# Third phase of a hybrid encoder trunk: order of one load, engine of one copy, place of two projections

## The chip, the cores and the metric

The kernel runs on one core of one Trainium2 chip. The metric is the device time of one execution in microseconds (us), the median of the runs shown. A core has five engines that each work through their own list of instructions: TensorE (PE in the profile, matmuls and transposes into PSUM; its weight loads are listed as PEld), VectorE (DVE), ScalarE (ACT), GpSimd (POOL) and SyncE (SP, which here issues most of the transfers). They wait for one another by semaphores.

## The reference

Two independent sequences of 1024 tokens with 1024 channels go through one layer with the same weights. The layer normalises its input, projects it to four branches (a gated linear recurrence, chunked gated linear attention "GLA", chunked gated DeltaNet, and a diagonal complex state-space model "S5"), mixes the four results with sigmoid gates and projects them back. The part that matters here is GLA and S5. GLA, cut to its core, for each of four heads and both directions:

```python
b = jnp.cumsum(log_a, axis=2)                      # log_a from a rank-16 projection of the input
q_dec, k_inv = q * jnp.exp(b), k * jnp.exp(-b)
scores = jnp.where(causal, q_dec @ k_inv.T, 0.0)   # inside a chunk
o_intra = scores @ v
S = de * S + k_end.T @ v                           # state carried from chunk to chunk
o = o_intra + q_dec @ S
o = rms_norm(o, norm_g) * silu(gate)
```

q, k, v and the gate are column blocks of one projection of the normalised input. S5 runs a complex linear scan over the sequence for 32 groups of channels; the kernel does it in real arithmetic after turning each state by a precomputed rotation.

## The kernel before, in words

The sequences are handled one after the other (`s` = 0, 1), each in four phases. A phase opens PSUM banks and buffers of its own and weaves several Python generators together. The weave (`weave`) gives every generator a position between 0 and 1; it always advances the one that lies furthest back, and a generator moves on by the number it yields, divided by its declared total. So a generator that yields less reaches its later parts earlier among the others.

The order that this writes is not yet the order on the engines. The framework takes the written order as a priority, runs a planning model of the engines over it, and fixes each engine's list for good: at each step the earliest written instruction that the plan holds to be ready. On the chip an engine keeps to its list, and stands still when the instruction in front is not ready, whatever lies behind it. Buffers are handed out in the same pass; a new user of a buffer waits for the last reader of the old one.

Every projection is done in float32 precision by three passes: a weight block is loaded (`raw`, two buffers), ScalarE rounds it (`hi`), GpSimd subtracts (`lo`), and TensorE adds up hi*hi, lo*hi and hi*lo products. `hi` and `lo` have four buffers each; one projection of 128 columns uses two, `values` (256 columns) all four. Results go to three PSUM banks called `pj`.

The third phase weaves three things: `gla` (declared total 18), `s5_core` (total 8, one unit for each of eight groups of four) and blocks of merge-gate projections for later ("gate blocks", `early`), six (first sequence) or seven (second) from position 0.3 on and seven from 0.85 on, each of 16 steps with three matmuls.

`gla` treats two pairs of heads (`pr` = 0, 1). Before the loop it projects q and k of the first pair (`qk(0)`) and starts the decays of the first direction. For each pair it then scales q and k of both directions by their decays (`scaled`), projects v (`values`: eight blocks of 128 tokens, each evacuated from its `pj` bank into the tile `vt`), builds the states for each direction (`states`: transposes of the scaled keys into a `gl` bank, a ScalarE copy to `kT`, the products of `kT` and `vt`, and VectorE's chain over the chunks into `Sm`), and forms the outputs (`outputs`: scores, mask, products, ScalarE copies). `ends` normalises the pair's outputs; for the first pair this is finished after the second pair's decays have begun. Its gate is loaded into a buffer with the tag `vt`, of which there is one, so the second pair's `vt` can be written only after the last read of that gate, the second `Sm<-gl,gla_ng,vt`. Between `states` and `outputs` of the first pair stand q and k of the second (`yield from qk(1)`), and the decays that follow.

q and k have one buffer each. `s5_core` loads, for each group of four, `uT` (the input, two buffers), `tin` (input weights, one buffer) and `E` (rotation and decay, two buffers), multiplies on TensorE into two `s5` banks (`head`), turns and scans on VectorE with products on GpSimd (`scan`), and multiplies back one group later (`tail`, a bank that ScalarE empties with a gelu into `zt`).

Nearly all instructions stand under line L54 in the profile, that of the helper that passes a call on, so they are told apart by tile names. Transfers have lines of their own: L1265 `uT`, L1266 `tin`, L1267 `E`, L202 weights.

Of the kernel before, what the change touches and what calls it, by code (L numbers as in the profile page):

```python
# [33 lines left out]
def tile_hybrid_trunk(ctx: ExitStack, tc: tile.TileContext, A):  # L34
# [28 lines left out]
    V, S, G, PE = Line(nc.vector, False), Line(nc.scalar, False), Line(nc.gpsimd, False), Line(nc.tensor)  # L63
    dma = nc.sync.dma_start
# [12 lines left out]
    def bank(tag):  # L77
        return ps["pool"].tile([128, 512], F32, tag=tag, bufs=ps["nb"][tag], name=nm(tag))
# [17 lines left out]
    def mm(*a, **kw):  # L96
        PE.matmul(*a, **kw)

    def transpose(*a):
        PE.transpose(*a)  # L100
# [4 lines left out]
    def tt(eng, out, a, b, op):  # L105
        eng.tensor_tensor(out, a, b, op)
# [7 lines left out]
    def stt(out, a, s, b, o1, o2):  # L114
        V.scalar_tensor_tensor(out, a, s, b, o1, o2)

    def bc(ap, n):
        return ap.unsqueeze(ap.ndim).to_broadcast(list(ap.shape) + [n])
# [4 lines left out]
    def nm(p):  # L123
        cnt[0] += 1
        return f"{p}{cnt[0]}"
# [103 lines left out]
    def run(gen):  # L229
        for _ in gen:  # L230
            pass
# [69 lines left out]
    def proj_cm(*a):  # L301
        run(proj_steps(*a))

    def proj_tok(xn, wp, src, c0, toks, evac):

        ws = wcols(wp, src, 0, 8, c0, 256)
        for i, tsl in enumerate(toks):
            p = bank("pj")
            n = 0
            for k in range(8):  # L310
                wh, wl = ws[k]
                xh, xl = xn[k][:, 0, tsl], xn[k][:, 1, tsl]
                for a, b in ((xh, wh), (xh, wl), (xl, wh)):
                    mm(p[:, :256], a, b, start=(n == 0), stop=(n == 23))
                    n += 1
            with soon():
                evac(i, p[:, :256])
# [554 lines left out]
    def gla(s, xn, ms, wp, pl):  # L872

        wt = lambda shape, tag, dt=F32: pl.tile(shape, dt, tag=tag, name=nm(tag))

        def qk(pr):
            q, k = wt([128, T], "q"), wt([128, T], "k")
            for t_, c0 in ((q, GLA_Q), (k, GLA_K)):
                def ev(hf, sl, p, t_=t_):
                    S.copy(t_[:, sl], p)  # L880
                proj_cm(xn, wp, w_in, c0 + pr * 128, 128, ev)
                yield
            return q, k

        def values(pr):
            vt = wt([128, 8, 256], "vt")

            def evv(i, p):
                V.tensor_copy(vt[:, i], p)
            proj_tok(xn, wp, w_in, GLA_V + pr * 256,  # L890
                     [slice(c * 128, (c + 1) * 128) for c in range(NT)], evv)
            return vt
# [34 lines left out]
            stt(q_, q, 0.125, Ab, ALU.mult, ALU.mult)  # L927
            return q_, k_, sm

        def states(d, k_, vt, sm):  # L930

            kT = wt([128, 8, 128], "kT")
            for g4 in range(2):
                p = bank("gl")
                for c in range(4):
                    cc = g4 * 4 + c
                    transpose(p[:, c * 128:(c + 1) * 128], k_[:, cc * 128:(cc + 1) * 128], ident)
                S.copy(kT[:, g4 * 4:g4 * 4 + 4], p.rearrange("p (c n) -> p c n", c=4))
            yield 0.4

            Smd = wt([128, 8, 128], f"Sm{d}")
            own = (slice(0, 4), slice(4, 7)) if d == 0 else (slice(4, 8), slice(1, 4))
            for cg in own:
                p = bank("gl")
                for c in range(cg.start, cg.stop):
                    for h in range(2):
                        o = (c - cg.start) * 128
                        mm(p[h * 64:(h + 1) * 64, o:o + 128], kT[:, c, h * 64:(h + 1) * 64],
                                  vt[:, c, h * 128:(h + 1) * 128], start=True, stop=True)
                n = cg.stop - cg.start  # L950
                sh = 1 if d == 0 else -1
                tt(V, Smd[:, cg.start + sh:cg.stop + sh], p[:, 0:n * 128].rearrange("p (c n) -> p c n", c=n),
                   bc(sm[:, 2, cg], 128), ALU.mult)
            for i in range(1, NT - 1):
                c = i if d == 0 else 7 - i
                cn = c + 1 if d == 0 else c - 1
                stt(Smd[:, cn], Smd[:, c], sm[:, 1, c:c + 1], Smd[:, cn], ALU.mult, ALU.add)
            use_c = slice(1, 8) if d == 0 else slice(0, 7)
            tt(V, Smd[:, use_c], Smd[:, use_c], bc(sm[:, 0, use_c], 128), ALU.mult)
            yield 0.4  # L960
            return Smd
# [44 lines left out]
            return [norm_out(pl, "gl", [ot[h]], gla_ng, sg[:, h], (s, 1, pr * 2 + h), wt([128, T], f"Sm{h}"),  # L1006
                             ot[h].rearrange("p c n -> p (c n)")) for h in range(2)]

        q, k = yield from qk(0)
        last = None  # L1010
        ab = decay(0, 0)
        yield 0.3
        for pr in range(2):
            one = scaled(0, q, k, *ab)
            ab = decay(1, pr)
            yield 0.3
            if last:
                for e in last:
                    run(e)
                yield 0.3  # L1020
            two = scaled(1, q, k, *ab)
            vt = values(pr)
            yield 2
            Sm = []
            for d, x in enumerate((one, two)):
                Sm.append((yield from states(d, x[1], vt, x[2])))
            if pr == 0:
                q, k = yield from qk(1)
                ab = decay(0, 1)
                yield 0.3  # L1030
            ot = yield from outputs((one[0], two[0]), (one[1], two[1]), Sm, vt)
            last = ends(pr, ot)
            for e in last:
                next(e)
            yield 0.3
# [8 lines left out]
    rot_d = dr.tile([NQ, 128, 3, 4, 128], F32, name="rot_d")  # L1044
# [16 lines left out]
    def s5_rot(rot, pl):  # L1061

        for qd in range(NQ):
            gs = slice(qd * 4, qd * 4 + 4)
            eng = V if qd % 2 == 0 else G
            E = pl.tile([128, 3, 4, 128], F32, tag="E", name=nm("E"))
            V.memset(E[:, 0, :, 0:1], 1.0)
            V.memset(E[:, 1, :, 0:1], 0.0)
            V.tensor_copy(E[:, 0:2, :, 1], rot[:, 0:3:2, 0, gs])
            for lv in range(1, 7):  # L1070
                m = 1 << lv
                both = [128, 2, 4, m]
                e, f = E[:, 0:2, :, 0:m], E[:, 0:2, :, m:2 * m]
                y = E[:, 2].rearrange("p a n -> p (a n)")[:, 0:8 * m].rearrange("p (r a n) -> p r a n", r=2, a=4)
                tt(eng, f, e, bc(rot[:, 0, lv, gs].unsqueeze(1).to_broadcast([128, 2, 4]), m), ALU.mult)
# [181 lines left out]
    def s5_core(s, xn, wp, pl):  # L1257
# [3 lines left out]
        def load(qd):  # L1261
            uT = wt([128, 4, 128], "uT", 2)
            tin = wt([128, 4, 2, 128], "tin")
            E = wt([128, 3, 4, 128], "E", 2)
            dma(uT, u_d[s, qd // 2, qd % 2 * 4:qd % 2 * 4 + 4].rearrange("g x c -> x g c"))  # L1265
            dma(tin, tin_d[qd])  # L1266
            dma(E, rot_d[qd])  # L1267
            return tin, uT, E

        def head(qd, tin, uT, E):  # L1270
# [308 lines left out]
    for s in range(nseq):  # L1579
        if s:  # L1580
            xn = last_part(s - 1, mg, me)
        with ExitStack() as br:
            fp = pool(f"fg{s}", 1, stack=br)
            bp = pool(f"bp{s}", 1, stack=br)
            with ExitStack() as st:
# [75 lines left out]
                pr = {}  # L1661
# [87 lines left out]
```

## Time and profile before

| what | value |
|---|---|
| median of 3 runs | 3104.76 us (3102.79 to 3108.0) |
| the profiled execution | 3103.76 us, its span 3101.5 us |
| mean granted TensorE clock | 0.966 of full speed |
| PE busy | 2875.3 us, 93% of the span |
| DVE busy | 1877.1 us, 61% |
| ACT busy | 1286.2 us, 41% |
| POOL busy | 1043.0 us, 34% |

[...] In a timeline, the bracket behind a row is the time that the engine stood idle before it, and what ended the wait. A name such as `vt<-pj` is the tile written and the tile read. The third phase's GLA lies at about 670 to 1010 us in the first sequence and 2145 to 2530 us in the second.

### The profile page before, as it was taken

Reading aid. Unit: us, or ns where it says so; the run is one execution under the profiler, and the core shown is the slowest. Engines: PE = TensorE matmul, PEld = TensorE weight load, DVE = VectorE, ACT = ScalarE, POOL = GpSimd, SP = SyncE. Lnnn points to the kernel's source line nnn. Section 1 sums busy time; section 2 is a strip of 40 time slices with the busy share of each in tenths; the row PEclk is TensorE's granted clock in tenths of the full one; section 3 lists DMA queues with packets and bytes.
Section 4 is the critical chain, followed back from the end, with each engine's and each line's share of the span. In section 5 each row is a group of like instructions: output and inputs, shape, how many; then the busy total and the mean of one; then the engine's idle time right before and its main releaser. Section 6 shows DMA issues by size and latency. Waiting matters only on the chain. (4 is left out here: it accounts for less than half of the span.)

```text
span 3101.5 us, 42101 instructions
## 1 busy us (share of the span) xinstructions
PE 2875.3 (93%) x15386; PEld 2373.6 (77%) x15386; DVE 1877.1 (61%) x3569; ACT 1286.2 (41%) x1969; POOL 1043.0 (34%) x796
## 2 busy tenths in 40 slices
PE   6999979898989999999999998989897999999998
PEld 5787767677778787878778876767776887788877
DVE  7576887738662464665654467773867245566545
ACT  5644546534432432332444465553443233333223
POOL 2343565434332231121443333343433212211123
PEclk9999989999999999999999998999998999999999
DMA  5344535353332754553553342524333263565343
GB/s 111 102 153 142 153 104 182 92 162 121 121 112 74 214 162 157 176 194 124 182 160 109 102 137 73 165 80 160 117 120 104 74 192 104 183 216 192 105 156 124
DMA packets 449391, 427.37 MB, mean 138 GB/s; under 512 B 126848, under 2 KB 340384, under 8 KB 449184
## 3 DMA queue, kind: packets, MB, share of 16 engines
q1 hardware_dynamic: 403200, 374.07, 39.2%
q10 hardware_dynamic: 45984, 50.61, 4.7%
q8 instruction: 121, 1.98, 0.3%
q14 instruction: 86, 0.70, 0.1%
HBM read 306.87 MB, written 117.70 MB: 137 GB/s over the span
## 5 line engine op out<-in xcount | busy, mean ns | idle before, releaser
L54 PE MATMUL pj<-xn,hi 128*128 128x512 f32 x4608 | 1471.2, 399 | 20.2 <-ACT y L54 5.7
L54 POOL TENSOR_TENSOR lo<-raw,hi 128x512 fp32r<-128x512 f32 x432 | 600.9, 1394 | 1451.8 <-ACT hi L54 1298.3
L54 PEld LDWEIGHTS pj<-xn,hi 128*128 128x128 f32 x4608 | 869.7, 191 | 206.1 <-ACT y L54 6.1
L54 PE MATMUL pj<-xn,lo 128*128 128x512 f32 x2304 | 912.5, 396 | 1.3 <-POOL lo L54 1.3
L54 ACT CAST hi<-raw 128x512 fp32r<-128x512 f32 x432 | 265.2, 618 | 650.8 <-PE pj L54 482.2
L54 PEld LDWEIGHTS pj<-xn,lo 128*128 128x128 f32 x2304 | 439.5, 191 | 99.5 <-issue 5.0
L54 ACT ACT_TABLE_LOAD x201 | 257.9, 1283 | 118.2 <-DVE Ab L54 54.6
L54 PE MATMUL pj<-yh,hi 128*128 128x512 f32 x576 | 239.8, 417 | 4.5 <-ACT yh L54 4.4
L54 PE MATMUL pj<-yl,hi 128*128 128x512 f32 x576 | 225.8, 393 | 1.0 <-DVE yl L54 1.0
L54 PE MATMUL pj<-yh,lo 128*128 128x512 f32 x576 | 226.0, 393 | 0.0
L54 DVE TENSOR_TENSOR_SCAN w<-E,v 64x512 f32<-64x512 f32 x64 | 97.9, 1529 | 85.2 <-PE s L54 84.3
L54 DVE TENSOR_TENSOR sg<-sg,pj 128x512 f32<-128x512 f32 x128 | 87.6, 684 | 93.4 <-PE pj L54 65.6
L54 PE MATMUL pj<-hi,mh 128*128 128x512 f32 x384 | 124.3, 400 | 6.7 <-ACT mh L54 4.1
L54 PEld LDWEIGHTS pj<-yh,hi 128*128 128x128 f32 x576 | 109.6, 190 | 23.9 <-ACT yh L54 5.2
L54 PEld LDWEIGHTS pj<-yh,lo 128*128 128x128 f32 x576 | 108.7, 189 | 23.8
L54 PEld LDWEIGHTS pj<-yl,hi 128*128 128x128 f32 x576 | 109.5, 190 | 19.9 <-DVE yl L54 2.6
L54 ACT ACTIVATE fg<-pj,bmg 128x512 f32<-128x512 f32 x112 | 76.3, 687 | 116.4 <-PE pj L54 104.2
L54 ACT ACTIVATE vn<-r,beta 128x128 f32<-128x128 f32 x128 | 40.7, 365 | 169.5 <-DVE vs L54 167.3
L54 POOL TENSOR_TENSOR dcv<-dcv,dsg 128x1024 f32<-128x1024 f32 x24 | 60.4, 2518 | 144.3 <-ACT dsg L54 103.5
L54 PE MATMUL pj<-hi,xn 128*128 128x256 f32 x512 | 97.9, 290 | 10.0 <-DVE vt L54 10.0
L54 DVE TENSOR_TENSOR yl<-yr,yh 128x512 fp32r<-128x512 f32 x80 | 59.9, 753 | 76.3 <-ACT yh L54 76.1
L54 DVE SCALAR_TENSOR_TENSOR dcv<-dup,dn_cw,dcv 128x1024 f32<-128x1024 f32 x72 | 96.0, 1333 | 5.5 <-ACT dcv L54 2.5
(373 smaller groups left out, 4469.1 us busy)
## 6 DMA issues: line engine op xcount, KB each, us to landing
raw<-in_w_in_dram SPq DMA_DIRECT2D x176, 256.0 KB, 2.9
sl<-rows_d SPq DMA_DIRECT2D x128, 256.0 KB, 6.5
raw<-in_w_merge_gate_dram SPq DMA_DIRECT2D x128, 256.0 KB, 2.9
gs_d<-fg ACTq DMA_DIRECT2D x112, 256.0 KB, 2.1
sg<-gs_d SPq DMA_DIRECT2D x112, 256.0 KB, 2.7
sl<-qkv_d SPq DMA_DIRECT2D x40, 512.0 KB, 5.5
raw<-in_w_branch_dram SPq DMA_DIRECT2D x64, 256.0 KB, 3.4
yr<-ysp SPq DMA_DIRECT2D x64, 256.0 KB, 3.1
```

The costliest lines, as they stand in the source:

```text
L54: i = f(*a, **kw)
```

## The change

Three edits in the third phase. `qk` puts its two tiles on a list instead of returning them, and for the first pair an iterator over `qk(1)` is handed to `states`, which advances it once for each direction, after the transposed keys have been copied out and before its own yield: q of the second pair is projected there in the first direction, k in the second. These steps yield nothing to the weave. The loop runs what is left of the iterator where `yield from qk(1)` stood; the sum of what `gla` yields falls from 19.1 to 17.1. `values` evacuates with a ScalarE copy instead of a VectorE copy. In `load`, E is requested first.

```diff
+        qks = []
+
         def qk(pr):
...
-            return q, k
+            qks.append((q, k))
...
             def evv(i, p):
-                V.tensor_copy(vt[:, i], p)
+                S.copy(vt[:, i], p)
...
-        def states(d, k_, vt, sm):
+        def states(d, k_, vt, sm, ahead):
...
                 S.copy(kT[:, g4 * 4:g4 * 4 + 4], p.rearrange("p (c n) -> p c n", c=4))
+            next(ahead, None)
             yield 0.4
...
-        q, k = yield from qk(0)
+        yield from qk(0)
+        q, k = qks[0]
...
+            ahead = qk(1) if pr == 0 else iter(())
             for d, x in enumerate((one, two)):
-                Sm.append((yield from states(d, x[1], vt, x[2])))
+                Sm.append((yield from states(d, x[1], vt, x[2], ahead)))
             if pr == 0:
-                q, k = yield from qk(1)
+                run(ahead)
+                q, k = qks[1]
                 ab = decay(0, 1)
                 yield 0.3
...
+            dma(E, rot_d[qd])
             dma(uT, u_d[s, qd // 2, qd % 2 * 4:qd % 2 * 4 + 4].rearrange("g x c -> x g c"))
             dma(tin, tin_d[qd])
-            dma(E, rot_d[qd])
```

## Rows read from the trace of the kernel before

**Rows 1.** The page's busy line: us, share of the span, instructions.

```profile
PE 2875.3 (93%) x15386; PEld 2373.6 (77%) x15386; DVE 1877.1 (61%) x3569; ACT 1286.2 (41%) x1969; POOL 1043.0 (34%) x796
```

**Rows 2.** Busy time by stretches of the third phase, with columns.

```profile
core 0: us, PE busy (x) PEld busy (x) DVE busy (x) ACT busy (x) POOL busy (x), PEclk, DMA share, GB/s
670.00:865.00 195.00, 184.91 (x1112) 156.39 (x1112) 131.62 (x218) 81.65 (x110) 74.14 (x45) 0.97 0.36 112
865.00:885.00 20.00, 10.62 (x55) 10.39 (x56) 19.67 (x30) 5.01 (x7) 7.75 (x4) 0.66 0.53 170
885.00:1057.00 172.00, 171.83 (x982) 144.00 (x981) 71.86 (x145) 47.62 (x71) 45.47 (x32) 1.00 0.40 127
2340.00:2375.00 35.00, 13.19 (x84) 12.61 (x85) 33.42 (x58) 6.48 (x8) 13.73 (x8) 0.72 0.42 140
```

**Rows 3.** PE's waits, whole span: total us, times, longest.

```profile
PE gl L54 <- ACT kT L54: 10.4, 2, 5.2
PE s L54 <- DVE t L54: 5.8, 2, 2.9
```

**Rows 4.** Timeline of PE, first sequence, first pair's states: start, us, what.

```profile
737.39 0.69 PE L54 MATMUL gl<-vt,kT 128*64 128x128 f32 x2 [5.21 <-ACT kT L54]
738.01 3.45 PE L54 MATMUL s<-uT,tin 128*128 128x128 f32 x16
753.70 0.49 PE L54 MATMUL s<-uT,tk 128*128 128x128 f32 x2 [2.91 <-DVE t L54]
```

**Rows 5.** Groups on PE from 727.7 to 737.3 us.

```profile
L54 PE MATMUL pj<-xn,hi 128*128 128x512 f32 x14 | 4.4, 396 | 0.0
L54 PE MATMUL pj<-xn,lo 128*128 128x512 f32 x6 | 2.3, 391 | 0.0
```

**Rows 6.** Timeline of ACT before that wait ends.

```profile
717.89 0.70 ACT L54 ACTIVATE Rl<-gl,gla_bn 128x512 f32<-128x512 f32 x1
...
736.26 0.60 ACT L54 ACTIVATE zt<-s 128x512 f32<-128x512 f32 x1
736.76 0.58 ACT L54 COPY kT<-gl 128x512 f32<-128x512 f32 x1
```

**Rows 7.** Stretches behind two of the waits, columns as in rows 2.

```profile
735.00:740.00 5.00, 2.61 (x11) 2.29 (x12) 4.96 (x4) 3.33 (x5) 3.80 (x2) 0.50 0.21 54
880.00:885.00 5.00, 4.41 (x23) 4.41 (x24) 4.76 (x14) 0.00 (x0) 0.00 (x0) 0.57 0.51 157
```

**Rows 8.** Timeline of DVE, then PE, first sequence, between the pairs.

```profile
874.66 1.41 DVE L54 SCALAR_TENSOR_TENSOR Sm<-gl,gla_ng,vt 128x512 f32<-128x512 f32 x2
875.99 2.02 DVE L54 TENSOR_TENSOR ki<-k,Rl 128x1024 f32<-128x1024 f32 x1
...
880.13 1.07 DVE L54 COPY vt<-pj 128x256 f32<-128x256 f32 x3
...
880.59 0.58 PE L54 MATMUL pj<-hi,xn 128*128 128x256 f32 x1 [5.45 <-DVE vt L54]
```

**Rows 9.** The same place in the second sequence, DVE, then PE.

```profile
2370.08 2.01 DVE L54 TENSOR_TENSOR ki<-k,Rl 128x1024 f32<-128x1024 f32 x1
2372.01 1.07 DVE L54 COPY vt<-pj 128x256 f32<-128x256 f32 x3
...
2358.18 0.76 PE L54 MATMUL s<-uT,tk 128*128 128x128 f32 x2 [15.02 <-issue]
```

**Rows 10.** The copies' forms: duration ns min/median/max, first and last start.

```profile
L54 DVE COPY vt<-pj x32: 390/417/425, 706.7 to 2388.7; 128x256 f32<-128x256 f32 x32
L54 ACT COPY qd<-gl x16: 349/373/374, 818.9 to 2510.6; 128x256 f32<-128x256 f32 x16
```

**Rows 11.** E's issues and time to landing, and the first product of the inputs.

```profile
L1267 SPq DMA_DIRECT2D E<-rot_d x16: 319/320/1114, 636.8 to 2352.0; - x16
DMA to landing us min/median/max: 3.5/4.3/10.4
L54 PE MATMUL s<-uT,tin x256: 270/275/582, 681.8 to 2367.2; 128*128 128x128 f32 x128
```

## The prediction
> **What bounds the kernel.** I read the page's busy line first, then PE's busy time and granted clock by stretches, then PE's waits, and last the timelines around the longest waits. TensorE is busy 93% of the span [rows 1], so the end moves only by what PE stands idle or runs at half clock. In the third phase the reader should see three kinds of stretch [rows 2]. From 670 to 865 us, pair 0 of the first sequence, PE has 184.91 of 195 us. At the border between the pairs it falls apart: 10.62 of 20 us at clock 0.66 in the first sequence, 13.19 of 35 us at 0.72 in the second, with DVE busy 19.67 and 33.42 us. After the border, from 885 to 1057 us, PE has 171.83 of 172 us, and there nothing can be gained. Two of PE's waits come once in each sequence with the same length [rows 3]: 10.4 us in two for `kT`, 5.8 us in two for the S5 scan. VectorE and ScalarE count only where PE waits for them.
>
> The order on each engine is fixed beforehand from the written order and planned times. So an edit has two effects: what a thing costs, and where the plan puts it. The second I can only bound.
>
> **v evacuated by ScalarE.** 32 copies leave VectorE at 0.417 us and come to ScalarE at 0.373 us, the price of a copy of the same shape out of PSUM [rows 10]: 13.3 us of VectorE, 11.9 us of ScalarE. ScalarE is busy 41% [rows 1], and a copy is hidden as long as a `pj` bank is free, so only places where PE waits count.
>
> First sequence, between the pairs [rows 8]: the last read of the old gate, which frees `vt`, ends at 874.66 + 1.41 = 876.07 us. The copies start at 880.13 us, behind two long VectorE instructions for the second direction, and PE goes on at 880.59 us after 5.45 us idle. ScalarE has finished its last `kT` copy by then and could copy at 876.07: 4.06 us saved. Second sequence [rows 9]: the buffer is free at about 2370.1 us, where `ki` starts, and the copies start at 2372.01 us: 1.9 us saved. Behind the first gap PE runs 4.41 busy us at clock 0.57 [rows 7], which loses about 0.43 x 4.41 = 1.9 us; with the gap cut to some 1.4 us I take half of that back, 1.0 us.
>
> Against it: in pair 0 the copies of late v blocks fall into ScalarE's chain for the second direction's decay, which runs without a gap from before 717.89 us [rows 6]. Two of them add 2 x 0.373 = 0.75 us, and VectorE loses one copy of 0.417 us from the same chain further down: +0.33 us, in each sequence +0.7 in all if PE feels it. What waits behind a v copy on ScalarE is the `kT` copy, the gelu and the roundings of weights. Sum: -4.1 - 1.9 - 1.0 + 0.7 = -6.3 us. If ScalarE turns out as late as VectorE was, it is +0.7; if the clock comes back wholly, -7.2.
>
> **q and k between transposed keys and products.** The work is the same, 2 x 48 matmuls in each sequence; it moves ahead of two waits. In pair 0 PE does the transposes, then 20 gate matmuls in the free time (14 + 6, some 4.6 us, 0.23 us each) [rows 5], then stands 5.21 us until `kT` [rows 4], which ScalarE copies at 736.76 us because `zt`, the gelu of S5's tail, goes at 736.26 us after the decays' exponentials [rows 6]. After it PE runs at clock 0.50 [rows 7]: the 16 input products at 738.01 take 3.45 us [rows 4], 1.5 to 1.9 us lost. One projection is 48 x 0.23 = 11 us, more than the 9.8 us (4.6 + 5.21) between the transposes and `kT`. If PE does all of q first, the gap and its clock go: 5.2 + 1.9 = 7.1 us per sequence, 14.2 us in all.
>
> What is late next: the input products of the next S5 group are written before the transposes, so they keep precedence over q. They need the bank that `zt` empties at 736.26 + 0.60 = 736.86 us. If the plan holds that bank to be free as early as now, PE reaches them after 20 matmuls as before and waits till 736.9: 0.5 us gained where 5.2 went. And the tail at 753.70 us waits 2.91 us for VectorE's scan [rows 4]; its end does not come earlier, so what PE gains before it is lost there, unless k, also 11 us, stands in front of it. From both sides the edit is worth 0 to -14.2 us for the `kT` gap, and at most -5.8 us more for the tails [rows 3]. The nearest rows are those of the same waits, and they show both releases (ScalarE at 736.86, VectorE at 753.7) untouched, so I take a value near the lower end: 2.5 us per sequence, -5.0 us.
>
> The q and k tiles have one buffer each; their new contents can be copied only after the second direction's scaling has read the old. That comes before the scan that the tail waits for, within q's 11 us, and two of the three banks hold both halves meanwhile: 0, at worst about one copy, 0.6 us as for `kT` [rows 6].
>
> **The fall of the yielded sum from 19.1 to 17.1.** All of `gla` after `qk(1)` comes 2/18 = 0.11 of the phase earlier against S5 and the gate blocks: about one S5 group and one gate block of 11 us move behind the border. Between the first outputs and the second values I count two gate blocks before and after, so the border has as much cover as it had. The second sequence's border stands 21.8 us idle (35 - 13.19) against 9.4 us (20 - 10.62) in the first [rows 2], 15.02 us of it before one S5 tail [rows 9]: it may fall to the first's pattern, -12.4 us, or not. I take 0, as nothing in the code decides it.
>
> **E first.** E lands 4.3 us after its issue (3.5 to 10.4) [rows 11]; ahead of `uT` and `tin` it can delay these by that much, but at the phase's start they are issued with E, near 636.8 us, and first used at 681.8 us [rows 11]. Later each of the three waits for its own buffer. No engine's wait ends with E's landing, so nothing is gained: 0, with up to 10 us of delay inside 40 us of cover.
>
> **Sum.** -6.3 - 5.0 = -11.3 us. The profiled execution took 3103.76 us, 2.26 us of it outside the span of 3101.5; it lies 1.0 us under the median. 3103.8 - 11.3 = 3092.5, on the median's scale 3093.5 us.
>
> **Rivals.**
>
> *The stall only moves (no change).* For it: PE's order follows planned times, and the releases that it waits for, `zt` and the scan, are not moved; v's gain at the border may be taken by the S5 scan that is now written ahead of the second direction's scaling. Against: the 4.06 us at the border is VectorE's queue and nothing else. 3104.8 - 2 = 3103 us.
>
> *The border closes too.* The second sequence's border falls to the first's pattern, -12.4, and q takes half of its upper end, -7.1, beside v's -6.3: 3104.8 - 25.8 = 3079 us. For it: both borders run the same code, and one is 12.4 us shorter. Against: VectorE is busy 33.42 of 35 us there and loses only copies of 0.417 us.
>
> *The cover is missing later (slower).* Pair 1 had a gate block written among its transposes and products; `gla` now passes there 0.11 earlier, so transposes and products of pair 1 stand without a block between them, as in pair 0 before. PE was without idle time there [rows 2]. If each sequence gets pair 0's `kT` gap with its clock there, 7.1 us, and the tail's 2.9 us [rows 4], that is +20.0, with v's -6.3 and q's 0: 3104.8 + 13.7 = 3118.5 us. It decides once the plan puts the products within less than 9.8 us of work behind the transposes. Against: seven gate blocks from 0.85 on are there to be drawn forward, and the decays of pair 1 are over by then, so ScalarE is freer. [...]
>
> **How the numbers follow.** A measurement here can tell about 0.2%, 6.2 us, from no change. Forecast (3086 to 3098) 0.40, border closes too 0.17, stall moves 0.26, slower 0.17. Faster by over 6.2 us: the first two, 0.57; within it 0.26; slower 0.17. The lower end takes in the upper bounds of the known waits, -7.2 - 14.2 - 12.4 = -33.8, rounded: 3072. The upper end goes half-way into the slower case, 3112, and leaves out about 0.15 in all. The likeliest case's own range is 3086 to 3098.
>
> **What would show it.** Right: no `vt<-pj` copy on VectorE, PE's wait for it at both borders under 2 us, and PE's `kT` waits gone in pair 0. If instead PE waits before `s<-uT,tin` or longer before the tail, the stall moved. Slower would show as new PE waits above 1 us after the border, where there were none. A wait of PE for `uT` that grows by some 4 us would make E's place matter. The forecast is wrong if PE's idle time in the third phase falls by less than 5 or more than 20 us, or if what it falls by comes back elsewhere.

## The result, and the profile after

The change made the kernel slower: 3121.72 us median (3117.36 to 3128.51, 4 runs) against 3106.38 us (3102.79 to 3108.57, 4 runs), a ratio of 1.0051 [1.0037, 1.0064], some 16 us. The forecast was 3093.5 us.

TensorE's busy line, against [rows 1], shows 20 us more busy time for the same 15386 matmuls, and VectorE not busier:

```profile
PE 2895.9 (93%) x15386; PEld 2389.1 (76%) x15386; DVE 1874.5 (60%) x3537; ACT 1290.6 (41%) x1997; POOL 1040.5 (33%) x796
```

The third phase of the profile after by stretches, columns as in [rows 2], PEclk being the granted TensorE clock as a share of full speed (this execution, the slowest of the four, is some 6 us late already when the phase begins):

```profile
670.00:860.00 190.00, 174.83 (x1022) 145.11 (x1021) 119.45 (x176) 78.61 (x112) 65.99 (x39) 0.96 0.33 104
860.00:900.00 40.00, 23.21 (x170) 22.60 (x169) 38.96 (x65) 10.01 (x15) 16.45 (x9) 0.79 0.43 138
900.00:1060.00 160.00, 160.00 (x882) 133.69 (x882) 59.26 (x102) 44.00 (x68) 44.10 (x32) 1.00 0.30 98
2340.00:2390.00 50.00, 31.87 (x221) 30.82 (x221) 46.24 (x80) 13.58 (x19) 17.33 (x9) 0.76 0.40 133
```

The reader is to see that most of the new idle time lies at the first sequence's border: TensorE has 23.21 of 40 us there at clock 0.79, while VectorE is busy 38.96. Behind the border PE has 160 of 160 us, as before. Idle time is only one side of the account: the 20 us of the busy line are the other, and most of the net loss lies there (the section on the second reading).

PE's waits after (total us, times, longest). The waits for `kT` [rows 3] are gone; the second row shown is the tail's, 12.7 us where it was 5.8:

```profile
PE s L54 <- issue: 17.9, 2, 13.0
...
PE s L54 <- DVE t L54: 12.7, 2, 6.4
...
PE gl L54 <- DVE qd L54: 9.9, 1, 9.9
...
PE s L54 <- ACT zt L54: 6.2, 2, 3.1
...
PE pj L54 <- ACT vt L54: 5.5, 2, 2.9
```

PE's timeline in the first sequence, only rows that follow a wait. The first three are pair 0 (for [rows 4]), the last three the border (for [rows 8]):

```profile
742.86 2.01 PE L54 MATMUL s<-uT,tin 128*128 128x128 f32 x8 [3.12 <-ACT zt L54]
...
759.60 0.77 PE L54 MATMUL s<-uT,tk 128*128 128x128 f32 x2 [6.37 <-DVE t L54]
...
815.29 1.19 PE L54 MATMUL gl<-Sm,qd 64*128 64x128 f32 x4 [4.41 <-DVE sc L54]
...
879.59 0.76 PE L54 MATMUL s<-uT,tk 128*128 128x128 f32 x2 [12.99 <-issue]
...
886.58 2.02 PE L54 MATMUL s<-uT,tin 128*128 128x128 f32 x16 [1.18 <-DMA uT<-u_d]
...
891.65 0.39 PE L54 MATMUL pj<-hi,xn 128*128 128x256 f32 x1 [2.62 <-ACT vt L54]
```

In pair 0, 5.21 + 2.91 us of waiting became 3.12 + 6.37, and the outputs wait 4.41 us for `sc`, where before has no wait of over 0.8 us. At the border 4.15 + 5.45 us became 12.99 + 1.18 + 2.62. The 4.15 us stand in this row of before:

```profile
868.93 2.82 PE L54 MATMUL gl<-ident,ki 128*128 128x128 f32 x12 [4.15 <-DVE ki L54]
```

"issue" names nothing, but VectorE's timeline does. This is VectorE at that border after the change:

```profile
854.25 1.21 DVE L54 TENSOR_TENSOR qd<-qd,rs 128x1024 f32<-128x1024 f32 x1
...
855.46 8.07 DVE L54 TENSOR_TENSOR_SCAN w<-E,v 64x512 f32<-64x512 f32 x4
863.56 1.09 DVE L54 TENSOR_SCALAR rs<-ssn 128x8 int32<-128x8 int32 x1
864.57 5.69 DVE L54 TENSOR_TENSOR_SCAN Ab<-ones,Rl 128x128 f32<-128x128 f32 x8
...
870.18 0.14 DVE L54 CAST rs<-rs 128x8 f32<-128x8 int32 x1
...
873.22 0.16 DVE L54 CAST rs<-rs 128x8 int32<-128x8 f32 x1
...
878.22 1.28 DVE L54 TENSOR_TENSOR t<-E,s 128x512 f32<-128x512 f32 x2
...
882.49 1.22 DVE L54 TENSOR_TENSOR ki<-ki,rs 128x1024 f32<-128x1024 f32 x1
883.90 5.85 DVE L54 TENSOR_TENSOR_SCAN w<-E,v 64x512 f32<-64x512 f32 x4 [0.19 <-PE s L54]
```

and before:

```profile
855.29 1.53 DVE L54 TENSOR_TENSOR qd<-qd,rs 128x1024 f32<-128x1024 f32 x1
856.75 0.16 DVE L54 TENSOR_SCALAR ssn<-ssn 128x8 f32<-128x8 f32 x1
...
867.65 1.22 DVE L54 TENSOR_TENSOR ki<-ki,rs 128x1024 f32<-128x1024 f32 x1
868.79 5.84 DVE L54 TENSOR_TENSOR_SCAN w<-E,v 64x512 f32<-64x512 f32 x4
```

The normalisation of the second head (`ends`) is a chain of some 15 steps (`ssn`, `rs`), all but one of 0.14 to 0.2 us, then `ki<-ki,rs`, whose transposes PE needs. Before, the chain ran first and S5's scan came behind it. After, the scan of an S5 group (8.07 us) and its products stand in the middle of the chain. From the start of `qd<-qd,rs` to the end of `ki<-ki,rs` it takes 883.71 - 854.25 = 29.5 us, before 868.87 - 855.29 = 13.6 us. Some of that is the scans themselves: the four of S5 took 8.07 us here and 5.84 us before, the eight of the decays (`Ab`) 5.69 us and 2.7 us; every long one of them (2.13 to 3.42 us for S5 where the others took 1.21 to 1.22, 1.41 to 1.42 us for the decays where the others took 0.39 to 0.42) began beside a GpSimd instruction (last section). PE's 12.99 us end 0.09 us after one of VectorE's reads of the S5 banks (878.22 + 1.28 = 879.50). S5 stands later against GLA than before: the fourth `zt` of the phase starts at 861.27 us, just ahead of the border, where before it started at 826.97 us and the fifth at 864.81 us.

The profile before has the same picture at the other border, and it was there to be read: the 15.02 us of [rows 9]. They end 0.09 us after such a read of VectorE too, and the chain takes 28.8 us there (2333.28 to 2362.09). The change brought the second sequence's border to the first, not the other way round. The second's own shrinks from 22.2 us of waits (1.50 + 15.02 + 1.11 + 4.54) to 17.8 (9.94 + 4.95 + 2.90). Over the two sequences idle time thus hardly changes: +9.1 and -7.6 us in the table below.

### The profile page after: what moved, and what is told of

Same layout as the page of the kernel before. It is cut to its first block, busy times and chain, and to the rows that moved or that the text cites. A ratio compares the mean times of both kernels' runs of the same rounds, so it can differ in the third digit from the quotient of the medians.

```text
span 3126.5 us, 42086 instructions
## 1 busy us (share of the span) xinstructions
PE 2895.9 (93%) x15386; PEld 2389.1 (76%) x15386; DVE 1874.5 (60%) x3537; ACT 1290.6 (41%) x1997; POOL 1040.5 (33%) x796
## 5 line engine op out<-in xcount | busy, mean ns | idle before, releaser
L54 PEld LDWEIGHTS pj<-yh,hi 128*128 128x128 f32 x576 | 108.7, 189 | 24.3 <-ACT yh L54 5.7
```

The costliest lines, as they stand in the source:

```text
L54: i = f(*a, **kw)
```

## Experiments

Each experiment was run in five rounds beside the kernel before on the same chip. To find where a profile gains or loses, I took the time between two of TensorE's matmuls of fixed number, counted by start: from the 3300th to the 5600th (third phase, first sequence) and from the 10850th to the 13000th (second), with PE's idle time in it in brackets. Every kernel runs the same 15386 matmuls, and their order is the same around those two ends.

| kernel | edit | ratio to before [95%] | first (idle), us | second (idle), us |
|---|---|---|---|---|
| before | | | 421.7 (23.8) | 410.3 (38.2) |
| after | all three | 1.0051 [1.0037, 1.0064] | 438.8 (32.9) | 411.1 (30.6) |
| e1_v | v on ScalarE alone | 0.9965 [0.9952, 0.9978] | 414.9 (18.1) | 407.8 (36.1) |
| e2_E | E first alone | 0.9996 [0.9985, 1.0007] | 422.1 (24.3) | 411.9 (39.0) |
| e3_qk | q, k moved, yields gone | 1.0070 [1.0054, 1.0087] | 440.7 (34.3) | 415.5 (35.6) |
| e4_shift | yields gone, nothing moved | 1.0060 [1.0046, 1.0074] | 437.6 (28.7) | 414.0 (33.0) |
| e5_all_keep | all three, yields kept | 1.0006 [0.9995, 1.0017] | 424.0 (23.0) | 408.0 (38.4) |
| e6_qk_keep | q, k moved, yields kept | 1.0030 [1.0018, 1.0041] | 431.6 (28.1) | 408.9 (36.9) |
| e16_q_only | only q moved, kept | 1.0026 [1.0016, 1.0036] | 425.2 (26.6) | 414.1 (41.2) |
| e17_q_second | q into the second place | 0.9998 [0.9990, 1.0007] | 421.2 (23.4) | 409.1 (35.9) |
| e7_s5rate | after, S5 faster throughout | 1.0064 [1.0049, 1.0079] | 439.6 (27.1) | 413.8 (31.1) |
| e14_s5_back | after, S5 set back | 1.0062 [1.0050, 1.0075] | 438.1 (31.9) | 420.0 (38.5) |
| e15_gates_back | after, gate blocks set back | 1.0106 [1.0088, 1.0123] | 441.1 (36.5) | 423.0 (47.8) |
| e18_both_back | after, both set back | 1.0041 [1.0028, 1.0054] | 437.5 (35.0) | 411.5 (37.8) |
| e8_v_joint | e1 with one norm chain | 0.9922 [0.9908, 0.9936] | 413.5 (17.7) | 396.0 (23.4) |
| e9_all_joint | after with one norm chain | 1.0026 [1.0013, 1.0039] | 431.1 (25.6) | 409.0 (30.6) |
| e19_keep_joint | e5 with one norm chain | 0.9959 [0.9945, 0.9973] | 426.1 (22.4) | 393.7 (21.2) |
| e11_all_pair | after, two heads tied | 1.0070 [1.0058, 1.0082] | 442.8 (42.7) | 412.9 (41.3) |
| e12_v_joint_pair | e8, two heads tied | 0.9958 [0.9946, 0.9970] | 418.8 (25.0) | 402.9 (29.5) |
| e13_all_joint_pair | e9, two heads tied | 1.0032 [1.0021, 1.0043] | 435.4 (34.0) | 406.7 (32.9) |

### The parts of the change, one at a time

v alone:

```diff
-                V.tensor_copy(vt[:, i], p)
+                S.copy(vt[:, i], p)
```

> Only the v copies on ScalarE; the order on TensorE is that of before. Theory A (the loss comes from gla reaching its later parts 2/18 earlier, which puts S5's scans into the border between the pairs): this edit is innocent and gives its own 4 to 6 us at the two borders, ratio 0.998. Theory B (the place of q and k itself loses): the same, 0.998. Theory C (v copies on ScalarE hold up what is queued behind them): slower by 5 us or more, 1.002 or above.

It gained 0.35%, more than the 0.2% expected. PE's waits for `vt` at the two borders fell from 5.45 to 1.11 and from 4.54 to 2.44 us:

```profile
880.37 0.39 PE L54 MATMUL pj<-hi,xn 128*128 128x256 f32 x1 [1.11 <-ACT vt L54]
...
2368.20 0.39 PE L54 MATMUL pj<-hi,xn 128*128 128x256 f32 x1 [2.44 <-ACT vt L54]
```

E alone, in `load`:

```diff
+            dma(E, rot_d[qd])
             dma(uT, ...)
             dma(tin, tin_d[qd])
-            dma(E, rot_d[qd])
```

> Of the change only the rotation's load first. TensorE's and VectorE's lists stay those of before; only the order of three loads on SyncE's queue differs. All theories: within 0.1% of before, 3104 to 3110. If uT behind E is ever late, a wait of PE for uT of up to 4 us in each sequence, plus 0.1 to 0.25%.

Nothing, as expected; PE's waits for `uT` are 1.7 us against 1.5.

The yields alone: q and k stay where they were.

```diff
-                q, k = yield from qk(1)
+                g = qk(1)            # advanced to its end, nothing yielded
```

> q and k of the second pair stay in their old place and the v copies on VectorE, but the two projections yield nothing to the weave, so gla's later parts come 2/18 earlier as in the changed kernel. Theory A: 10 to 20 us slower, ratio 1.003 to 1.006, and the first sequence's border shows an idle stretch of TensorE above 10 us before an S5 tail. Theories B and C: no change, within 0.1%.

It lost 0.60% with not one instruction added or moved by hand, and its border is that of the change, 12.97 us where 4.15 stood, then v's wait, with v still on VectorE:

```profile
875.38 0.77 PE L54 MATMUL s<-uT,tk 128*128 128x128 f32 x2 [12.97 <-issue]
...
890.06 0.58 PE L54 MATMUL pj<-hi,xn 128*128 128x256 f32 x1 [4.76 <-DVE vt L54]
```

q and k moved without their yields, as in the change's diff, with v on VectorE and E last:

> Only the moved projections, with the sum at 17.1; v copied by VectorE, E last. Theory A and theory B: as slow as the changed kernel or slower by the v copies' gain, 1.005 to 1.007. Theory C: no slower than 1.002.

The worst of this group, 0.70%; v on ScalarE makes it better, not worse (0.51% with it), so ScalarE's queue is not the cause.

The whole change, with each moved projection yielding 1 as it did:

```diff
-            next(ahead, None)
-            yield 0.4
+            got = next(ahead, 0)
+            yield 0.4 if got == 0 else 1.4
```

> The whole change, but each of the two moved projections still yields 1 to the weave, so that the sum stays 19.1. Theory A: the loss goes, and the v copies' gain is left: 0.996 to 1.000. Theory B: the loss stays, 1.004 to 1.006. Theory C: 1.002 or above.

0.06% over before: 0.45% of the change's 0.51% goes with two numbers that draw other work forward. Theory A also expected v's gain to be left over (0.996 to 1.000); it is not, and the next runs say why. The border is before's again, with v's wait cured:

```profile
881.77 2.82 PE L54 MATMUL gl<-ident,ki 128*128 128x128 f32 x12 [3.93 <-DVE ki L54]
...
889.37 0.39 PE L54 MATMUL pj<-hi,xn 128*128 128x256 f32 x1 [0.96 <-ACT vt L54]
```

### The place of q and k

The same with v on VectorE and E last, so that only the place differs from before:

> Of the change only the place of the second pair's q and k; each of the two moved projections yields 1 to the weave as before (sum 19.1), v on VectorE, rotation's load last. Theory A (the loss comes from the shorter yielded sum, which puts S5's scan into the border's norm chain): border of s0 within 2 us of the 9.6 us of before, time within 0.15% of before, 3104 to 3112. Rival P (the moved place itself costs, as the pair of runs with v on ScalarE, 3096.3 without it and 3108.4 with it, hints): before plus 0.4%, about 3120, with a stall that before does not have.

0.30% slower, nearer to rival P's 3120 us than to theory A's 3112. I had called the place minor after the first four runs (e3 against e4, 0.10%); alone it is not. Which of the two places, q alone tells:

```diff
+            got = next(ahead, 0) if d == 0 else 0     # e16; e17: if d == 1
...
-                q, k = yield from qk(1)
+                yield from ahead
+                q, k = qks[1]
```

> Before, with only q of the second pair moved, between the first direction's transposed keys and their products (k at its old place, each yielding 1 as before). If the first direction's place is what costs (the kT wait of 5.2 us goes, and waits before S5's products and tail and the half clock behind them come in its place): between 0.1% and 0.3% over before, 3110 to 3116. If the second projection does it, in that both together push S5 and the states apart: within 0.1% of before or up to 0.3% under it, 3097 to 3109.

> Before, with q of the second pair moved into the second direction's place and k at its old one, each yielding 1. In that place of before TensorE has no wait of over 1 us for kT, so there is nothing to fill: within 0.1% of before, 3103 to 3110, if the first place is the costly one; 0.1 to 0.3% over before, 3110 to 3116, if the second is.

The first direction's place costs 0.26%, the second's nothing. PE's timeline of e16 in pair 0, rows behind a wait:

```profile
740.48 1.28 PE L54 MATMUL s<-uT,tin 128*128 128x128 f32 x8 [3.40 <-ACT zt L54]
...
757.30 0.76 PE L54 MATMUL s<-uT,tk 128*128 128x128 f32 x2 [5.66 <-DVE t L54]
...
777.01 0.66 PE L54 MATMUL gl<-ident,ki 128*128 128x128 f32 x4 [2.13 <-DVE Sm L54]
```

3.40 + 5.66 + 2.13 = 11.2 us, where before has 5.21 + 2.91 = 8.1 us: the difference is the 2.8 us by which e16's idle time grows in the table. PE does 22 matmuls of q between the transposes and the S5 products that wait for `zt`, where it did 20 of a gate block: q took the place of other cover, it added none. ScalarE's list is the same up to there. Then the rest of q, the S5 tail and 36 more projection matmuls stand ahead of most products with `kT` (770.76 us, where before has them from 737.39 us), so `Sm` is started later, and PE meets a new wait for it.

### What the dropped yields act through

S5's declared total raised, so that each of its yields counts for less (e7), and S5's position in the weave set back by 2/18 at the point where `qk(1)` had yielded (e14; both diffs are shortened):

```diff
-  weave((18, gla(s, xn, ms, wp, pl)), (8, s5_core(s, xn, wp, spl)),
+  weave((18, gla(s, xn, ms, wp, pl)), (9.7, s5_core(s, xn, wp, spl)),      # e7
```

```diff
         while live:
+            if jump[0]:
+                for x in live:
+                    if x[3] == 1:            # e14: S5; e15: > 1, the gate blocks; e18: > 0
+                        x[0] -= jump[0]
+                jump[0] = 0
...
                 run(ahead)
                 q, k = qks[1]
+                jump[0] = 2 / 18
```

> The whole change, with one number altered outside it: S5's declared total in the weave 9.7 in place of 8, so that S5's blocks stand against GLA's border about where they stood before; the yields of the moved projections stay gone. Theory A: the first half's border falls from 16.8 us to 4 to 8, time 3105 to 3114. Rival G (the shorter sum acts through the gate blocks of phase 3 or through everything behind it, not through S5's scan at the border): the border may go, the time stays within 0.15% of the whole change, 3120 to 3127.

> The whole change, but where the two yields of qk(1) stood before, S5's position in the weave is set back by 2/18, so that S5 stands against GLA as it did before; the gate blocks stay shifted. Theory A (the loss is S5's scan that the shorter sum lets fall into the border between the pairs): the first half's border falls from 16.8 us to under 8 us, the second's stays or shrinks, time 3108 to 3114, against 3122 to 3128 for the whole change and 3108 with both yields kept. Rival G (the gate blocks' shift costs): 3118 to 3128.

Both closed the first sequence's border as theory A said, 16.8 us to 5.7 us each, and neither became faster: the times, 3127.0 and 3127.3 us, are rival G's. The second border, 17.8 us in the change, has 19.5 us of waits in e14 and 13.6 in e7. e14, first sequence:

```profile
810.80 0.79 PE L54 MATMUL gl<-vt,sc 128*128 128x128 f32 x2 [4.39 <-DVE sc L54]
...
873.00 2.82 PE L54 MATMUL gl<-ident,ki 128*128 128x128 f32 x12 [4.38 <-DVE ki L54]
...
880.62 0.39 PE L54 MATMUL pj<-hi,xn 128*128 128x256 f32 x1 [1.32 <-ACT vt L54]
...
930.10 1.16 PE L54 MATMUL gl<-qd,ki 64*128 64x128 f32 x8 [2.16 <-DVE Sm L54]
```

The 4.39 us for `sc` stood in the change already (4.41). The 11.1 us that the border lost came back in small waits: 4.6 us in pair 1 (916 to 935 us: 1.31 + 2.16 + 1.16), where none was, 1.6 more before the tail in pair 0 (7.94), 0.9 for `sc`, and 4 at the phase's end. In e7 they stand early, 4.36 us for `vt` at 726.28 and 5.67 us for `Sm`. With the gate blocks set back and S5 left:

> The same, with the gate blocks set back by 2/18 at that place and S5 left shifted. Theory A: the scan still lies in the border, time 3118 to 3128. Rival G: 3106 to 3114.

the first border closed too (2.72 + 3.03 + 0.51 us), and S5's last group, with nothing left beside it, made PE wait at the phase's end in both sequences. The time, 3139.8 us, lies outside both expected ranges, so setting the gate blocks back (rival G) does not give the loss back either:

```profile
1049.61 0.79 PE L54 MATMUL s<-w,tout 128*128 128x128 f32 x2 [12.59 <-DVE w L54]
...
2561.05 0.80 PE L54 MATMUL s<-w,tout 128*128 128x128 f32 x2 [12.60 <-DVE w L54]
```

Both set back at the old place:

> The whole change, with S5 and the gate blocks both set back by 2/18 at the place where qk(1) yielded. Theory B (the loss is the balance of the three streams: with S5 alone set back the border closed and the stalls came before and behind it, with the gate blocks alone set back 12.6 us came at the phase's end, so only both together help): 3107 to 3115, near the 3108 of the kernel that yields in the moved places. Rival (the loss lies in pair 0, between the moved places and the border, where the weave is still shifted): 3118 to 3128.

0.41%, 3120.1 us, in the rival's range: behind the border this kernel keeps its distance to before exactly, as e5 does, but between the moved projections and the border it has lost more (7.96 us before the tail, 6.44 before outputs, 10.7 us at the border). So most of what e5 saves is saved by yielding at the place where the projections run.

### The chain at the border

If the border hangs on the norm's small steps, fewer of them should shorten it. One chain over 16 columns for both heads, instead of two over 8:

```diff
+                ssn = wt([128, 16], "ssn")
...
+                rstd = rsqrt_acc(pl, ssn, [128, 16], "n")
+                for h in range(2):
+                    tt(V, ot[h], ot[h], bc(rstd[:, h * 8:h * 8 + 8], 128), ALU.mult)
```

> v on ScalarE alone (3096.3), and the norm of GLA's two heads computed with one chain of small steps over 16 columns in place of two chains over 8: half as many of VectorE's small instructions between the border's last output and the next pair's keys. If that chain is what the border of s0 and s1 still waits for: 4 to 10 us less, 3086 to 3092. Rival (the chain is covered, or the first head's result now comes later and makes the transposes wait): 3096 to 3102.

> The whole change with the same joint norm chain, yields as in the change. If the loss of the change is S5's scan lying between the many small steps of the second head's norm (each step waits for a scan of 5 to 8 us): the border of s0 falls from 16.8 to under 8 us, time 3100 to 3112. If the scan's own time ahead of the keys is enough: border 10 to 15 us, time 3115 to 3124.

> The whole change with the moved projections' yields kept (3108.4) and the joint norm chain (12 us less when added to v on ScalarE alone, 7 less when added to the whole change). If the three effects add: 3095 to 3102. If the chain's gain stands against the moved projections, as under the shifted weave: 3101 to 3108. Either way above the 3084.4 of v on ScalarE with the joint chain and q and k in their old place, if moving them costs what it cost before (0.26% in the first direction).

A step over 16 columns takes as long as one over 8, 0.17 to 0.18 us against 0.16 to 0.17, so that one chain for both heads has half the steps at the same time each. Two rows of e8; over 8 columns the same two steps took 0.16 and 0.17 us in before (at 856.75 and 856.94 us):

```profile
857.86 0.18 DVE L54 TENSOR_SCALAR ssn<-ssn 128x16 f32<-128x16 f32 x1
858.07 0.17 DVE L54 TENSOR_SCALAR rs<-ssn 128x16 int32<-128x16 int32 x1
```

With v on ScalarE it gives the fastest kernel, 3084.36 us (3078.25 to 3086.70), 0.78% under before, better than both kernels of the case and than the 3086 to 3092 expected. The gain lies at the second sequence's border. The stretch 2330 to 2370 us, first e1 and then e8 (PE busy is the second number, the clock the third from the end):

```profile
2330.00:2370.00 40.00, 19.68 (x150) 18.86 (x149) 35.12 (x60) 12.29 (x16) 15.28 (x9) 0.79 0.38 122
```

```profile
2330.00:2370.00 40.00, 33.54 (x246) 32.13 (x246) 26.26 (x49) 14.74 (x23) 11.71 (x7) 0.87 0.28 95
```

In e1 the 14.97 us before the S5 tail are still there; in e8 none is over 4.07 us. VectorE does less in that stretch and PE more: the wait was the steps standing behind scans, and in e8 the joint chain runs with no scan in it (2329.28 to 2334.57 us). In the change the joint chain cures half (e9, 0.26% instead of 0.51%): the first border falls from 16.8 to 9.7 us, between the two expected figures, and the time, 3115.2 us, lies at the low end of the second. e19 gains a little more than the sum of the three: 3093.5 us where 3095 to 3102 was expected, 0.41% under before, and 0.37% above e8, near the 0.30% that the moved projections cost without the chain.

### A second reading: busy time and the order of the heads

Of the first half's 17.1 us only 9.1 are idle time; 8 us are busy time. Part of it is in GLA's products of 64 rows. Two rows of the kernel before:

```profile
926.34 1.16 PE L54 MATMUL gl<-qd,ki 64*128 64x128 f32 x8
...
954.91 1.16 PE L54 MATMUL gl<-qd,ki 64*128 64x128 f32 x16
```

After, no block of scores is of the second kind; one at about the same place:

```profile
965.83 1.16 PE L54 MATMUL gl<-qd,ki 64*128 64x128 f32 x8
```

Where the two heads alternate on the list, 16 take as long as 8 of one head, 1.16 us; the kernel has one head in partitions 0 to 63 of `qd` and `ki`, the other in 64 to 127 (`hp`). The trace names no head. That the order on the list decides is read from e11 below, which ties the heads in alternating order: 14 of its products take 1.16 us too. This is a row of e11:

```profile
948.04 1.16 PE L54 MATMUL gl<-qd,ki 64*128 64x128 f32 x14
```

With them one behind the other, all eight score blocks of a sequence take 16.3 us after (from one start to the next), 13.4 and 11.3 us before. The products of `qd` with the states (`gl<-Sm,qd`) have 64 rows too: 16.1 and 13.1 us after, 12.2 and 12.5 us before.

Both sequences of the large table added up show how much hangs on this. Busy is time less idle; "64 rows" is the time of scores and state products, from one start to the next without idle time; "alternating" counts the score products, of 256, that start within 20 ns of the one before.

| kernel | idle, us | busy, us | 64 rows, us | alternating |
|---|---|---|---|---|
| before | 62.0 | 770.0 | 49.4 | 62 |
| after | 63.5 | 786.4 | 61.8 | 0 |
| e4_shift | 61.7 | 789.9 | 62.5 | 0 |
| e5_all_keep | 61.4 | 770.6 | 49.9 | 72 |
| e14_s5_back | 70.4 | 787.7 | 62.1 | 13 |
| e15_gates_back | 84.3 | 779.8 | 49.7 | 96 |
| e18_both_back | 72.8 | 776.2 | 49.0 | 88 |

Of the 17.9 us that the change adds here, 16.4 are busy time, and 12.4 of these lie in the 64-row products. e4 loses the alternation with the yields alone, e5 has it back with them. So the largest cost of the dropped yields is that TensorE's list no longer alternates the heads (62 score products and 28 state products that no longer start together, 0.11 us each, the median time from one start to the next within a score block of after, make 9.9 us, an estimate); the first sequence's new idle time is about made up for in the second. With the gate blocks set back (e15, e18) the alternation returns. With S5 alone set back (e14) it does not, so that closing the border left the busy time where it was. But e15 and e18 stand idle more, and lose some 12 and 11 us more than before to half clock (granted clock of the profiled execution 0.961 and 0.964, in before 0.966). Why the plan drops the alternation was not followed up.

I tied the heads in alternating order, in the scores and in the state products alike:

```diff
+            line[0] = nm("pair")      # each on PE behind the one before
             for j in range(2):
...
+            line[0] = 0
```

> The whole change, and the score products and state products of GLA's two heads tied in alternating order on TensorE's list, so that neighbours use different halves of the array's rows. Theory H (half of the loss is that the earlier GLA lists one head behind the other: 16 records of gl<-qd,ki take 1.96 to 2.17 us where the alternating list of before takes 0.99 to 1.09 us): gl<-qd,ki falls from 16.3 us in each sequence's third phase to 8 or 9, gl<-Sm,qd from 16.1 and 13.1 to about 10, together 12 to 22 us less: 3100 to 3110. Rival (the records only look shorter, or the tie makes TensorE wait for the second bank): within 0.2% of the whole change, 3116 to 3128.

> v on ScalarE, the joint norm chain (3084.4 without the tie), q and k and the yields as before, and the same tie of the two heads. Theory H: before has 3 of 8 score blocks alternating in the first sequence (13.4 us in 8 blocks) and more in the second (11.3 us), so 3 to 5 us each from the scores and 2 to 4 us from the state products: 3068 to 3076. Rival: the tie costs as much in waits for banks as it saves, 3081 to 3090.

> The whole change with both the joint norm chain and the tie. If the border's chain (theory A) and the order of the heads (theory H) are the two things that the shorter yielded sum costs, the two cures add: 3115 minus 12 to 22, 3093 to 3103, under before. If they overlap or a third cost stands behind them: 3105 to 3116.

The busy time fell by 5.8 and 8.9 us in e11, from 405.9 to 400.1 and from 380.5 to 371.6, 14.7 us in all, and the scores to 10.5 and 10.2 us. Idle time rose by 9.8 and 10.7 us: TensorE's list, disturbed again, waits longer for the same VectorE chain:

```profile
868.52 1.94 PE L54 MATMUL gl<-ident,qd 128*128 128x128 f32 x8 [6.83 <-DVE qd L54]
...
893.86 0.77 PE L54 MATMUL s<-uT,tk 128*128 128x128 f32 x2 [15.12 <-issue]
```

None of the three gained; e12 (3095.9 us) and e13 (3118.5 us) lie above both of their expected ranges. The tie gives back what the lost alternation costs, but changes the lists otherwise too, so these runs do not show the change with the alternation alone restored.

## Why the prediction was wrong

**The failed step: the fall of the yielded sum, taken as 0 "as nothing in the code decides it".** It costs 0.45% inside the change (e5 to after, 14 us) and 0.60% by itself (e4). With it fell the premise that "the end moves only by what PE stands idle or runs at half clock": TensorE did the same matmuls in 16.4 us more of busy time, 12.4 of them in the 64-row products of the two heads, which no longer alternate, while idle time as a whole grew by 1.5 us. The prediction had no term for that. On the idle side, I counted gate blocks between outputs and values, found as many as before, and stopped there. The S5 group that the same paragraph puts behind the border was not followed onto VectorE, which was busy 19.67 of 20 us there [rows 2]: an engine with no room, and a chain of small steps for the scan to fall into. The sentence that the second border "may fall to the first's pattern" had the right pattern and the wrong direction: the first border got the second's.

**q and k moved: -5.0 forecast, +0.30% (9 us) measured.** "If instead PE waits before `s<-uT,tin` or longer before the tail, the stall moved": it did, to those two places. The first rival named that mechanism, and its releases, but priced it at nothing. Each of the two waits it named is priced in e16; the third, for `Sm`, I had not seen: the rest of q delays the products that VectorE's chain starts from. I had bounded this edit at zero from below though it puts 11 us of work ahead of a chain.

**v on ScalarE: -6.3 forecast, -0.35% (10.9 us, interval 6.8 to 14.9) measured.** Right in its places (4.34 and 2.10 us of the two waits, 4.06 and 1.9 forecast) and a little small. Of the 9.3 us that the two stretches of the table gain, 7.8 are idle time and 1.5 busy time, where the clock term stood at 1.0. The term with the wrong sign is the +0.7: in e1 the waits for `kT` and for the tail shrink by 1.5 us in all (5.21 to 4.94 in both sequences, 2.91 to 2.67 and 2.85 to 2.10). Its reading was wrong as well: ScalarE's chain does not run "without a gap from before 717.89 us", as ScalarE stands idle for 7.73 us until 731.01 us. The copies behind v in ScalarE's list did not hold PE up in e1, where the waits for `kT` are the shorter ones.

**E first: 0 forecast, -0.04% [-0.15, +0.07] measured.** Right.

**The sum.** The parts, measured singly, add up: -0.35 + 0.30 - 0.04 + 0.60 = 0.51%, the change's own figure (with 0.45 for the yields it is 0.36; each has some 0.13 of uncertainty). That they meet is partly luck: moved projections and dropped yields together cost 0.70% (e3), not 0.30 + 0.60.

**The slower rival** came near in time (3118.5 us) by another road. It saw the missing cover in pair 1's `kT` and tail, behind the border; PE had 160 of 160 us there. The cover was missing at the border and in pair 0, and what made pair 1 slower was busy time. That the time fits is luck.

**Open.** What the yields cost is settled, and so is where it lies in the traces: in busy time, chiefly the lost alternation. Half of the change's loss also goes with a shorter chain (e9), which saves idle time (63.5 to 56.2 us) and leaves the 64-row products at 60.8 us. Which rule of the plan drops the alternation is open, and so is what a list would cost that has the alternation, the short waits and the full clock at once: each way of setting a stream back left the first sequence at 437 to 441 us, e7 and e14 with most of the alternation lost, e15 and e18 with more idle time and more half clock.

## What to carry to other kernels

In a weave that is turned into fixed lists, a yield is a price: it says how much of the others' work is drawn beside this step, and moving a step without its yield is an edit to everything behind it; keep the yield first, and time the move and the yield apart. Where one engine is full and another waits for a chain of many small steps on it, ask which long instruction of a third party can be listed between them; fewer steps (here two chains made one, 0.43% on top of v) was worth more than any other place for the work. The same matmuls need not take the same busy time (here 16.4 us more in the two stretches of the third phase): compare busy and idle time apart, before looking for the cause among the waits. And busy time saved on an engine can come back as idle time, as it did with the tie (14.7 us saved in e11, 20.5 us of new idle time).

## What the runs showed of the hardware

The score products over 64 rows ran two at a time where the lists alternate the two heads: 16 took 1.16 us (before, 954.91 us), as long as 8 that follow one another in one head (926.34 us). In before 62 of 256 started within 20 ns of the one ahead of them; in after none did, and the median start there is 0.11 us behind the one ahead. I had not known that the kernel's lists had both forms, nor that the change had lost one of them.

One scan of an S5 group took 1.21 to 1.22 us or, with the same shape, 2.05 to 3.42 us. In the traces of before and after, with 64 such scans each, all 45 long ones (21 and 24) began while a GpSimd instruction was running, and ended 1.07 to 1.09 us after it; the other 83 began with none running. Three rows of after, the fast scan and then a slow one with the GpSimd instruction beside it:

```profile
858.88 1.22 DVE L54 TENSOR_TENSOR_SCAN w<-E,v 64x512 f32<-64x512 f32 x1
860.04 2.41 POOL L54 TENSOR_TENSOR Rl<-Rl,Ab 128x1024 f32<-128x1024 f32 x1 [2.28 <-ACT Ab L54]
860.10 3.42 DVE L54 TENSOR_TENSOR_SCAN w<-E,v 64x512 f32<-64x512 f32 x1
```

So these scans look as if they waited for GpSimd's instruction to end, which is a reading of the two traces and not shown, as no run varied it; the 3.42 us stand as VectorE's busy time.
